# Attention scores: every product over 128 rows, the first block as two f32r products

## The chip, the cores and the metric

The kernel runs on one core of a Trainium2 chip. The metric is the time of the whole program on the device, in microseconds (us). Of three runs of the kernel before, the median was 1330.12 us (1329.44 to 1330.89).

## The reference, cut to what matters

Two layers, each with three token mixers on 512 tokens of width 1024. One of the mixers is a stick-breaking attention with 8 heads of 64 columns, in blocks of 128 queries; query block `blk` sees the keys of all blocks up to its own:

```python
def stick_breaking(q, k, v, q_norm, k_norm):
    q = rmsnorm(q, q_norm)
    k = rmsnorm(k, k_norm)
    for blk in range(S_ // SB_BLOCK):
        z = einsum('bqhd,bkhd->bhqk', q[:, start:end], k[:, :end]) * scale
        causal = s_idx[None, :] < t_idx[:, None]
        log_keep = where(causal, log_sigmoid(-z), 0.0)
        after = cumsum(log_keep, axis=3, reverse=True) - log_keep
        w = where(causal, exp(log_sigmoid(z) + after), 0.0)
        outs.append(einsum('bhqk,bkhd->bqhd', w, v[:, :end]))
```

The change concerns `z` alone, the scores.

## The kernel before, in words

**Main work.** The weights come as 196 units of 128 x 1024 floats. Each is split into a high part `wh` (ScalarE rounds it to f32r, L316) and a low part `wl` (VectorE subtracts, through the helper at L197), and the activations likewise (`hh`, `hl`). A product of matrices is then three f32r products per step: high by high, high by low, low by high. Nearly all main products (tile `mm`) have 128 rows, 128 stationary columns and 512 moving columns. They are issued in pieces of 24 products, in an order written out by hand.

**The order around the change.** Everything else is a set of generators that are advanced between or behind the pieces: at a piece's start those that are due go one step (ScalarE, VectorE and POOL work is issued there), then the piece's products are issued, and a generator that yielded 0 goes on behind the piece; there it issues its own products. Each engine works through its own queue in the order of issue. A budget per piece, counted from the columns of the products issued, decides how much background work (the preparation of the third mixer, on VectorE and POOL) is issued with it.

**The attention.** `sb_pair` treats two heads (a pair) whose 64 columns lie on rows 0 to 63 and 64 to 127 of the tiles `sq` and `sk` (named `sqk` in the trace). At its start it makes, for each head h: `qd[h]`, the high part of q, by ScalarE on the head's own 64 rows and copied by POOL (a cast, L1029) to the other 64 rows; `ks[h]`, the high part of k on the head's own rows (ScalarE) and the low part on the other rows (VectorE); and the low part of q in one tile `ql` for both heads, each on its own rows (VectorE). A product of `qd[h]` with `ks[h]` over all 128 rows is so q-high by k-high plus q-high by k-low; the product of `ql` with the high rows of `ks[h]`, over 64 rows, adds q-low by k-high. `scores` (L1032) does this for blocks 1 to 3. For block 0 it takes one plain float32 product of q and k over the head's 64 rows, which shows as two records. Behind each block's products a bf16 product of `identb` and `negm` adds -1e30 above the diagonal: the mask.

Per head the scores of block 3 are issued in one place (tile `z3`, with 512 columns of keys) and those of blocks 0, 2 and 1 one or two pieces later (`z02`, `z1`, with 128, 384 and 256 columns). `weights_of` turns the scores into weights: two sigmoids by ScalarE (`kp`, `w`), scans and a product by VectorE (L1051 and L197). `turn` transposes the weight blocks through TensorE (tile `wt`, L1068), ten per head; the first is from block 0, the second from block 1. The values are then added up in `sbo`, products with 64 output columns that alternate between the two heads' halves. Pairs start four pieces apart, so that the copies of one pair are made while the pair before it has the scores of its second head.

The trace names a product out<-moving,stationary. All tiles named z (`z3`, `z02`, `z1`) show as `z`.

Of the kernel before, what the change touches and what calls it, by code (L numbers as in the profile page):

```python
# [10 lines left out]
F32 = mybir.dt.float32  # L11
F32R = mybir.dt.float32r
BF16 = mybir.dt.bfloat16
AF = mybir.ActivationFunctionType
ALU = mybir.AluOpType
# [171 lines left out]
def trunk(ctx: ExitStack, tc, x_in, w_in, par_in, bc_in, ng_in, cst_in, rope_in, out):  # L187
    nc = tc.nc
    load = {"V": 0.0, "G": 0.0, "T": 0.0}

    def counted(f, engine, each):


        def g(*a, **k):
            o = k["out"] if "out" in k else a[0]
            load[engine] += 0.07 * (engine != "T") + each * math.prod(o.shape[1:])
            return f(*a, **k)  # L197

        return g

    TT = counted(nc.vector.tensor_tensor, "V", 1.04e-3)
# [4 lines left out]
    MM = counted(nc.tensor.matmul, "T", 0.42e-3)  # L206
# [9 lines left out]
    def bt(name, dt=F32, shape=(P, 512)):  # L216
        return bp.tile(list(shape), dt, tag="b", name=name)
# [7 lines left out]
    def psm(name):  # L225
        return ps_sm.tile([P, 512], F32, tag="sm", name=name)
# [12 lines left out]
    def C(n):  # L239
# [7 lines left out]
        out=negm, in_=negm, pattern=[[1, P]], base=0, channel_multiplier=-1, compare_op=ALU.is_ge, fill=0.0  # L247
# [31 lines left out]
    def split(src, name, shape=(P, 512)):  # L279
        h = bt(name + "h", F32R, shape)  # L280
        l = bt(name + "l", F32R, shape)
        ACT(h, src, AF.Copy)  # L282
        TT(out=l, in0=src, in1=h.bitcast(F32), op=ALU.subtract)
        return h, l
# [523 lines left out]
    def layer(l, last, base):  # L808
# [206 lines left out]
        def sb_pair(pr):  # L1015
            w02, w3 = [None] * 2, [None] * 2
            qf, kf = sq[pr], sk[pr]
            half = [slice(0, 64), slice(64, 128)]

            qd = [bt("qd0", F32R), bt("qd1", F32R)]  # L1020
            ks = [bt("ks0", F32R), bt("ks1", F32R)]
            ql = bt("ql", F32R)
            for h in range(2):
                r, o = half[h], half[1 - h]
                ACT(qd[h][r, :], qf[r, :], AF.Copy)  # L1025
                ACT(ks[h][r, :], kf[r, :], AF.Copy)
                TT(out=ql[r, :], in0=qf[r, :], in1=qd[h][r, :].bitcast(F32), op=ALU.subtract)
                TT(out=ks[h][o, :], in0=kf[r, :], in1=ks[h][r, :].bitcast(F32), op=ALU.subtract)
                nc.gpsimd.tensor_copy(out=qd[h][o, :], in_=qd[h][r, :])  # L1029
            yield K["b1"]  # L1030

            def scores(ps, off, h, b):  # L1032
                n = 128 * (b + 1)
                c = slice(b * P, b * P + P)
                r = half[h]
                if b == 0:
                    MM(ps[:, off : off + n], qf[r, c], kf[r, 0:n], start=True, stop=False)
                else:
                    MM(ps[:, off : off + n], qd[h][:, c], ks[h][:, 0:n], start=True, stop=False)
                    MM(ps[:, off : off + n], ql[r, c], ks[h][r, 0:n], start=False, stop=False)  # L1040
                MM(ps[:, off + n - P : off + n], identb, negm, start=False, stop=True)

            def weights_of(ps, segs, sg):

                end = sum(segs[-1])
                kp = bt("kp")
                ACT(kp[:, 0:end], ps[:, 0:end], AF.Sigmoid, scale=-0.125)  # L1047
                ACT(sg, ps[:, 0:end], AF.Sigmoid, scale=0.125)
                for off, n in segs:
                    v = kp[:, off + 1 : off + n][:, ::-1]  # L1050
                    nc.vector.tensor_tensor_scan(v, v, zero1.to_broadcast([P, n - 1]), 1.0, ALU.mult, ALU.add)  # L1051
                TT(out=sg[:, 0 : end - 1], in0=sg[:, 0 : end - 1], in1=kp[:, 1:end], op=ALU.mult)

            w1 = bt("w1")
            wt0, wt13, wt2 = [None] * 2, [None] * 2, bt("wt2")

            def wblk(h, b, kb):
                c = kb * P + (128 if b == 2 else 256 * h if b == 1 else 0)
                return (w02[h], w1, w02[h], w3[h])[b][:, c : c + P]

            def turn(h):
                pts = []
                for blocks in (
                    [(b, 0) for b in range(4)], [(1, 1), (2, 1), (3, 1), (3, 3)], [(2, 2), (3, 2)],
                ):
                    pt = psm("wt")
                    for i, (b, kb) in enumerate(blocks):
                        nc.tensor.transpose(pt[:, i * P : i * P + P], wblk(h, b, kb), ident)  # L1068
                    pts.append(pt)
                return pts  # L1070

            def turned(h, pts):
                wt0[h], wt13[h] = bt("wt0"), bt("wt13")
                ACT(wt0[h], pts[0], AF.Copy)
                nc.vector.tensor_copy(out=wt13[h], in_=pts[1])
                ACT(wt2[:, 256 * h : 256 * h + 256], pts[2][:, 0:256], AF.Copy)

            for h in range(2):
                ps = psm("z3")
                scores(ps, 0, h, 3)  # L1080
                if h == 1:
                    pts = turn(0)
                yield 0
                w3[h] = bt("w3")
                weights_of(ps, [(0, 512)], w3[h])
                if h == 1:
                    turned(0, pts)
                yield K["b2"]
                ps, ps1 = psm("z02"), psm("z1")
                scores(ps, 0, h, 0)  # L1090
                scores(ps, 128, h, 2)
                scores(ps1, 0, h, 1)
                yield 0
                w02[h] = bt("w02")
                weights_of(ps, [(0, 128), (128, 384)], w02[h])
                weights_of(ps1, [(0, 256)], w1[:, 256 * h : 256 * h + 256])
                yield K["b3"]
            pts = turn(1)
            yield 0
            turned(1, pts)  # L1100
            yield K["b4"]
            po = psm("sbo")
            for kb in range(4):

                for h in range(2):
                    c = slice(128 * pr + 64 * h, 128 * pr + 64 * h + 64)
                    w = (wt0[h], wt13[h][:, 0:384], wt2[:, 256 * h : 256 * h + 256], wt13[h][:, 384:512])[kb]
                    MM(po[half[h], 128 * kb : 512], sv[kb][:, c], w, start=kb == 0, stop=kb == 3)
            yield 0
            sbo[pr] = bt("sbo")  # L1110
            nc.vector.tensor_copy(out=sbo[pr], in_=po)
            yield K["b5"]
            while zb[pr] is None:
                yield 1
            TT(out=sbo[pr], in0=sbo[pr], in1=zb[pr], op=ALU.mult)
            yb[pr] = split(sbo[pr], "yb")
# [207 lines left out]
        for i in range(4):  # L1324
            spawn(sb_pair(i), at["sv"] + 3 + K["sb0"] + K["sb_gap"] * i)
# [66 lines left out]
```

## Time and profile before

| what | value |
|---|---|
| median of three runs | 1330.12 us |
| the profiled execution | 1332.1 us |
| its span in the profile | 1330.4 us |
| instructions | 16615 |
| TensorE busy | 1299.4 us, 6360 products |
| VectorE busy | 854.5 us |
| ScalarE busy | 537.7 us |
| POOL busy | 371.3 us |
| mean granted clock of TensorE | 0.993 |

The profile is of one execution, which took a little longer than its span and than the median of the runs. Busy times are shares of the span. The end of a product is modelled in the profile, so that records of products that follow each other overlap; the start of one to the start of the next is what TensorE spends on it. An idle time in brackets, as in [1.66 <-DVE w L197], is how long the engine stood still before that row, and what ended it.

### The profile page before, as it was taken

What the parts mean: (1) busy time and instruction counts of PE and PEld (TensorE: products, weight loads), DVE (VectorE), ACT (ScalarE), POOL (GpSimd) and SP (SyncE); (2) the same over time, 40 slices, a digit from 0 to 9 for tenths busy, and PEclk for the clock granted to TensorE, in tenths of its full rate; (3) what the DMA queues carried; (4) which work ended last, traced back from release to release, by engine and by line L of the source; (5) the groups of instructions that cost most, each with busy time, mean ns of one, the idle gap of its engine ahead of it and who ended that gap; (6) DMA issues with size and microseconds to landing.
All of it is one profiled execution on the core that took longest, in us unless ns stands there. A gap on an engine that the chain in (4) does not pass through costs nothing. (4 is left out here: it accounts for less than half of the span.)

```text
span 1330.4 us, 16615 instructions
## 1 busy us (share of the span) xinstructions
PE 1299.4 (98%) x6360; PEld 1051.4 (79%) x6360; DVE 854.5 (64%) x1189; ACT 537.7 (40%) x919; POOL 371.3 (28%) x436
## 2 busy tenths in 40 slices
PE   7989989999999999999999999899999999999998
PEld 5867768788887888888888777688888878888887
DVE  5996677886686438555365566779647854485542
ACT  5345543535434434333234444344544444333311
POOL 3330035738443012000052000575465321120000
PEclk9999989999999999999999999899999999999999
DMA  6232221223321222224533221112242233223342
GB/s 220 85 125 77 64 64 30 94 68 96 100 91 64 95 80 73 86 91 139 166 113 125 79 65 64 48 64 80 80 127 64 64 94 97 79 64 95 95 131 75
DMA packets 37375, 120.05 MB, mean 90 GB/s; under 512 B 4144, under 2 KB 4528, under 8 KB 37296
## 3 DMA queue, kind: packets, MB, share of 16 engines
q1 hardware_dynamic: 29664, 105.40, 25.2%
q10 hardware_dynamic: 7632, 13.59, 3.0%
q8 instruction: 50, 0.82, 0.3%
q14 instruction: 29, 0.24, 0.1%
HBM read 114.78 MB, written 4.19 MB: 89 GB/s over the span
## 5 line engine op out<-in xcount | busy, mean ns | idle before, releaser
L197 DVE TENSOR_TENSOR wl<-raw,wh 128x1024 fp32r<-128x1024 f32 x196 | 250.4, 1287 | 122.1 <-ACT wh L316 120.0
L197 PE MATMUL mm<-hh,wh 128*128 128x512 f32 x640 | 256.7, 401 | 0.0
L197 PE MATMUL mm<-hh,wl 128*128 128x512 f32 x640 | 252.4, 394 | 2.3 <-DVE wl L197 2.3
L197 PE MATMUL mm<-hl,wh 128*128 128x512 f32 x640 | 250.5, 391 | 0.0
L316 ACT ACTIVATE wh<-raw 128x1024 fp32r<-128x1024 f32 x196 | 206.0, 1057 | 86.1 <-DVE wl L197 31.1
L197 PE MATMUL mm<-wh,hh 128*128 128x512 f32 x512 | 210.2, 411 | 0.9 <-ACT hh L419 0.9
L197 PE MATMUL mm<-wl,hh 128*128 128x512 f32 x512 | 205.3, 401 | 4.1 <-DVE wl L197 4.1
L197 PE MATMUL mm<-wh,hl 128*128 128x512 f32 x512 | 204.7, 400 | 0.0
L197 PEld LDWEIGHTS mm<-hh,wl 128*128 128x128 f32 x640 | 120.6, 188 | 30.3 <-DVE wl L197 3.6
L197 PEld LDWEIGHTS mm<-hh,wh 128*128 128x128 f32 x640 | 120.8, 189 | 24.9 <-issue 1.8
L197 PEld LDWEIGHTS mm<-hl,wh 128*128 128x128 f32 x640 | 120.7, 189 | 24.5
L197 PEld LDWEIGHTS mm<-wl,hh 128*128 128x128 f32 x512 | 104.8, 205 | 25.7 <-DVE wl L197 6.8
L197 PEld LDWEIGHTS mm<-wh,hh 128*128 128x128 f32 x512 | 104.6, 204 | 21.3 <-ACT hh L419 1.3
L197 PEld LDWEIGHTS mm<-wh,hl 128*128 128x128 f32 x512 | 104.5, 204 | 20.9 <-DVE hl L197 0.3
L1051 DVE TENSOR_TENSOR_SCAN kp<-kp,zero 128x511 f32<-128x511 f32 (+1 forms) x64 | 60.3, 963 | 35.6 <-ACT kp L1047 35.1
L992 ACT ACTIVATE gate<-mm 128x512 f32<-128x512 f32 x48 | 28.6, 596 | 119.7 <-PE mm L197 119.7
L197 POOL TENSOR_SCALAR ms<-ss 128x8 f32<-128x8 f32 (+3 forms) x56 | 19.2, 342 | 184.0 <-DVE ss L822 101.9
L1029 POOL CAST qd<-qd 64x512 fp32r<-64x512 f32 x16 | 15.8, 988 | 186.9 <-ACT qd L1025 172.0
L197 POOL TENSOR_TENSOR rs<-ms,mhalf 128x8 f32<-128x8 f32 (+3 forms) x56 | 64.7, 1155 | 4.7
L820 ACT ACTIVATE sq<-mm 128x512 f32<-128x512 f32 x32 | 19.0, 593 | 89.1 <-PE mm L197 89.1
L197 PE MATMUL mm<-wl,mgh 128*128 128x512 f32 x128 | 50.1, 391 | 0.2
L197 PE MATMUL mm<-wh,mgh 128*128 128x512 f32 x128 | 49.9, 390 | 0.0
(254 smaller groups left out, 2260.4 us busy)
## 6 DMA issues: line engine op xcount, KB each, us to landing
raw<-in_w SPq DMA_DIRECT2D x196, 512.0 KB, 3.5
x<-in_x SPq DMA_DIRECT2D x8, 256.0 KB, 7.3
rope<-in_rope ACTq DMA_DIRECT2D x8, 256.0 KB, 4.3
xh<-in_x ACTq DMA_DIRECT2D x8, 256.0 KB, 4.6
x<-xh ACTq DMA_DIRECT2D x8, 256.0 KB, 2.1
xh<-x ACTq DMA_DIRECT2D x8, 256.0 KB, 4.5
out<-xh ACTq DMA_DIRECT2D x8, 256.0 KB, 2.1
gB<-in_ng SPq DMA_DIRECT2D x2, 256.0 KB, 5.8
```

What stands on the lines that cost most here:

```text
L197: return f(*a, **k)
L316: ACT(wh, raw, AF.Copy)
L820: ACT(s2, ps, AF.Square)
L992: ACT(sg, ps, AF.Sigmoid)
L1029: nc.gpsimd.tensor_copy(out=qd[h][o, :], in_=qd[h][r, :])
L1051: nc.vector.tensor_tensor_scan(v, v, zero1.to_broadcast([P, n - 1]), 1.0, ALU.mult, ALU.add)
```

## The change

Instead of one tile `ql` for both heads there are two, `ql[0]` and `ql[1]`. Each holds the head's low part of q on the head's own 64 rows, as before, and zeros on the other 64, which a memset on POOL writes, issued ahead of the cast of the same head. The second product of a block then goes over all 128 rows of `ql[h]` and `ks[h]`; the rows with the low part of k meet the zeros. Block 0 is treated like the others: the plain float32 product over 64 rows is replaced by the two f32r products over 128 rows, with 128 columns. The mask products, the weights and what follows stay.

```diff
             qd = [bt("qd0", F32R), bt("qd1", F32R)]
             ks = [bt("ks0", F32R), bt("ks1", F32R)]
-            ql = bt("ql", F32R)
+
+            ql = [bt("ql0", F32R), bt("ql1", F32R)]
             for h in range(2):
                 r, o = half[h], half[1 - h]
                 ACT(qd[h][r, :], qf[r, :], AF.Copy)
                 ACT(ks[h][r, :], kf[r, :], AF.Copy)
-                TT(out=ql[r, :], in0=qf[r, :], in1=qd[h][r, :].bitcast(F32), op=ALU.subtract)
+                nc.gpsimd.memset(ql[h][o, :].bitcast(F32), 0.0)
+                TT(out=ql[h][r, :], in0=qf[r, :], in1=qd[h][r, :].bitcast(F32), op=ALU.subtract)
                 TT(out=ks[h][o, :], in0=kf[r, :], in1=ks[h][r, :].bitcast(F32), op=ALU.subtract)
                 nc.gpsimd.tensor_copy(out=qd[h][o, :], in_=qd[h][r, :])
             yield K["b1"]
...
                 n = 128 * (b + 1)
                 c = slice(b * P, b * P + P)
-                r = half[h]
-                if b == 0:
-                    MM(ps[:, off : off + n], qf[r, c], kf[r, 0:n], start=True, stop=False)
-                else:
-                    MM(ps[:, off : off + n], qd[h][:, c], ks[h][:, 0:n], start=True, stop=False)
-                    MM(ps[:, off : off + n], ql[r, c], ks[h][r, 0:n], start=False, stop=False)
+                MM(ps[:, off : off + n], qd[h][:, c], ks[h][:, 0:n], start=True, stop=False)
+                MM(ps[:, off : off + n], ql[h][:, c], ks[h][:, 0:n], start=False, stop=False)
                 MM(ps[:, off + n - P : off + n], identb, negm, start=False, stop=True)
```

## Rows read from the trace of the kernel before

**Rows 1.** The page, part 1: busy time, share, instructions of three engines.

```profile
PE 1299.4 (98%) x6360; PEld 1051.4 (79%) x6360; DVE 854.5 (64%) x1189; ACT 537.7 (40%) x919; POOL 371.3 (28%) x436
```

**Rows 2.** The waits of TensorE: total us, times, longest us.

```profile
PE wt L1068 <- DVE w L197: 8.1, 4, 2.4
PE mm L197 <- DVE wl L197: 6.3, 7, 1.5
PE z L197 <- DVE ks L197: 2.7, 1, 2.7
```

**Rows 3.** TensorE's timeline (start, duration): scores of blocks 0, 2, 1 of a head.

```profile
115.69 0.40 PE L197 MATMUL mm<-hh,wl 128*128 128x512 f32 x1
116.02 0.48 PE L197 MATMUL z<-sqk 64*128 64x128 f32 x2
116.44 0.23 PE L197 MATMUL z<-negm,identb 128*128 128x128 bf16 x1
...
116.82 0.44 PE L197 MATMUL z<-ks,ql 64*128 64x384 f32 x1
117.20 0.23 PE L197 MATMUL z<-negm,identb 128*128 128x128 bf16 x1
...
117.53 0.38 PE L197 MATMUL z<-ks,ql 64*128 64x256 f32 x1
117.84 0.23 PE L197 MATMUL z<-negm,identb 128*128 128x128 bf16 x1
...
118.19 0.39 PE L197 MATMUL mm<-hl,wh 128*128 128x512 f32 x1
```

**Rows 4.** TensorE's timeline: scores of block 3, and the transposes behind them.

```profile
123.24 0.39 PE L197 MATMUL mm<-hh,wl 128*128 128x512 f32 x1
123.47 0.40 PE L197 MATMUL z<-ks,qd 128*128 128x512 f32 x1
123.80 0.49 PE L197 MATMUL z<-ks,ql 64*128 64x512 f32 x1
124.22 0.23 PE L197 MATMUL z<-negm,identb 128*128 128x128 bf16 x1
124.29 1.26 PE L1068 MATMUL wt<-ident,w 128*128 128x128 f32 x10
125.31 0.48 PE L197 MATMUL mm<-hh,wh 128*128 128x512 f32 x1
```

**Rows 5.** TensorE's timeline: f32r products of 256 columns in the retention.

```profile
1169.51 0.28 PE L197 MATMUL ro<-rvsh,sTs 128*128 128x256 f32 x1
1169.62 0.28 PE L197 MATMUL ro<-rvsl,sTs 128*128 128x256 f32 x1
1169.74 0.28 PE L197 MATMUL ro<-rvsh,sTs 128*128 128x256 f32 x1
```

**Rows 6.** The timeline of all engines: POOL's memsets beside a VectorE product.

```profile
217.26 0.99 POOL L767 MEMSET mt<- 128x512 f32 x2
...
217.67 0.68 DVE L197 TENSOR_TENSOR sbo<-sbo,silu 128x512 f32<-128x512 f32 x1
```

**Rows 7.** VectorE's timeline from a pair's copies to the previous pair's last weights.

```profile
117.27 0.68 DVE L197 TENSOR_TENSOR ql<-sqk,qd 64x512 fp32r<-64x512 f32 x1 [3.38 <-ACT qd L1025]
117.98 0.98 DVE L197 TENSOR_TENSOR ks<-sqk,ks 64x512 fp32r<-64x512 f32 x1
...
120.01 0.69 DVE L197 TENSOR_TENSOR ks<-sqk,ks 64x512 fp32r<-64x512 f32 x1
...
123.46 0.42 DVE L197 TENSOR_TENSOR w<-w,kp 128x255 f32<-128x255 f32 x1
```

**Rows 8.** TensorE's timeline at a wait for the weights `w`.

```profile
190.93 0.30 PE L1068 MATMUL wt<-ident,w 128*128 128x128 f32 x1 [1.66 <-DVE w L197]
```

**Rows 9.** Two stretches: busy us (instructions) of PE, PEld, DVE, ACT, POOL; granted clock.

```profile
190.00:200.00 10.00, 6.66 (x21) 5.65 (x22) 8.36 (x8) 1.98 (x5) 4.83 (x5) 0.66 0.29 97
415.00:425.00 10.00, 7.97 (x35) 5.95 (x35) 9.73 (x8) 4.02 (x5) 5.08 (x3) 1.00 0.50 161
```

## Prediction, made before the change was built

> **What bounds the kernel now.** I read the page's busy times first: TensorE is busy for 98% of the span, VectorE for 64% [rows 1]. A busy share alone says little, since the ends of products are modelled, so next come TensorE's own waits: it waits for VectorE's `w` four times, for `wl` seven times, for `ks` once, 17.1 us in all [rows 2]; beyond these it waits only for the first input, at the start. Outside these places the order of TensorE's queue is the clock of the program, and a product that gets shorter moves everything behind it forward. So the price of a score product is not its recorded duration but the distance from its start to the next start, and I read those distances in the timeline of TensorE.
>
> In a run of main products the distance is 0.23 us. The scores of blocks 0, 2 and 1 of one head stand in [rows 3], those of block 3 in [rows 4]. There the reader is to see that every change between a 128-row and a 64-row product lengthens a distance. Into one: the last main product to the first `sqk` product 0.33 (115.69 to 116.02), `qd` of 512 columns to `ql` 0.33 (123.47 to 123.80): 0.10 more than 0.23. Out of one: `ql` of 512 columns to the mask 0.42 (123.80 to 124.22), 0.19 more; the plain product of block 0 (two records) to the mask takes 0.42, of which 0.22 are left for the product if the way out is 0.20. Products of 128 rows on both sides don't pay it: two f32r products of 256 columns in the retention start 0.11 to 0.12 apart [rows 5], and ten transposes of 128 columns take 1.02 us, 0.10 each [rows 4].
>
> **The change, part by part.** There are 16 heads (2 layers, 4 pairs, 2 heads), each with its four blocks of scores and a mask behind each. All prices are per head.
>
> *Block 3.* `qd` to `ql` to mask is 0.33 + 0.42 = 0.75 [rows 4]; with no change of rows it is 2 x 0.23 = 0.46. Saved: 0.29.
>
> *Block 0.* The plain product goes, two f32r products of 128 rows and 128 columns come. Before: 0.33 + 0.42 = 0.75 from the last main product to the mask [rows 3]. After: 0.23 for the main product, then two products whose price no row has. The lower end is 0.06 each, half of the 256-column distance [rows 5]; the upper end is 0.21 each, what the plain product of this size takes (0.42 less the way out). I take 0.10, from the transposes, which also have 128 stationary columns and 128 moving ones [rows 4]. After 0.43, saved 0.32; ends 0.40 and 0.10.
>
> *Block 2, 384 columns.* Mask to `ql` is 0.38 now (116.44 to 116.82) [rows 3]. A mask followed by a 512-column product of 128 rows takes 0.35 to the start after it (117.84 to 118.19), and 384 columns are 0.055 shorter (halfway between 0.12 and 0.23): 0.295, saved 0.085. `ql` to mask falls from 0.38 to 0.175, saved 0.205.
>
> *Block 1, 256 columns.* Mask to `ql` 0.33 to 0.24, saved 0.09; `ql` to mask 0.31 to 0.12, saved 0.19 [rows 3, 5].
>
> Sum: 0.29 + 0.32 + 0.085 + 0.205 + 0.09 + 0.19 = 1.18 us per head, 18.9 us over 16 heads.
>
> The weak point is the change out: after every 64-row product comes a mask in bf16, so no row parts the change of rows from the change of type. If the 0.19 to 0.20 belonged to the mask, four of them would stay and 1.18 would become 0.39. I take the rows as the cause, since the change in costs 0.10 with no change of type. The Trainium skill, TensorEngine Tiling (Array Packing), section Key Properties, says that changing the tiling mode (not just the tile) drains the engine; by that rule both directions go and the sum is the 18.9, without it as little as 6.2.
>
> *The memsets.* 16 of them, 64 x 512, on POOL, ahead of the cast of the same head. The nearest row is a 128 x 512 memset, two in 0.99 us [rows 6], so about 0.5 us each, 8 us in all on an engine that is busy for 28% [rows 1]. The first of a pair needs no input and runs while POOL waits for ScalarE; the second puts the second cast back by 0.5 us. Cost on TensorE: 0, because the first product that reads the cast stands a whole main piece (5 us) behind it, and the memset of a head ends before its cast, for which that product waits already. If that cover is gone it is 0.5 us per pair, 4 us. Does a memset slow VectorE, whose `ks` of 0.69 us takes 0.98 while POOL casts [rows 7]? Beside the two memsets a VectorE product of two tiles took 0.68 us [rows 6], undisturbed. So 0; the upper end is 0.3 us in each of the six places below, 2 us. The Trainium skill has both answers: GPSIMD Engine Reference, section Specifications, names contention with VectorE instructions of two SBUF inputs without saying which POOL instructions; SBUF — State Buffer, section Who interferes with whom, leaves out those that only write. The row is with the second; by the first the sum would be up to 2 us smaller.
>
> The number of VectorE's subtractions and of ScalarE's copies stays. Two of the `ql` products per head get 64 zero rows, which no row prices; a product's distance goes by columns in [rows 3 to 5], so 0. The background's budget counts one more product of 128 columns per head, 0.05 us against pieces of 5: 0, either way at most one small operation moved.
>
> **What is late next.** In every layer three of the four pairs make their copies (`qd`, `ks`, `ql`) just when the previous pair's second head has its block-0, -2 and -1 scores. VectorE then runs a closed chain: it starts when ScalarE has made `qd`, right behind the main piece, and goes through four subtractions, the scans and ends with `w` at 123.88 (123.46 + 0.42) [rows 7]. The transposes that read it start at 124.29, the second of them (which needs this `w`) at 124.39 [rows 4]: about 0.43 us of slack. The chain's start hangs on the main piece, not on the scores, so TensorE comes 1.18 us earlier and waits 1.18 - 0.43 = 0.75. There are four such places, alike in the two layers: 3.0 us given back. At the last pair of each layer POOL's background runs beside this chain, and TensorE waits there already: two waits per layer, 8.1 us in all [rows 2], the first of them in [rows 8]. That is 1.18 more per layer, 2.4 us. The first block 3 of the first layer stands between waits for `ks` and `wl` [rows 2], set by VectorE: its 0.3 is lost. At the last head of each layer one of the waits for `wl` [rows 2] ends a VectorE chain that starts at the mask of block 2, so what is saved behind that mask, 0.3, is lost: 0.6. Given back: 3.0 + 2.4 + 0.3 + 0.6 = 6.3 us.
>
> Net: 18.9 - 6.3 = **12.6 us**. The profiled execution took 1332.1 us, 1.7 above its span and 2.0 above the median of the runs; it would be 1319.5, and the median 1330.1 - 12.6 = **1317.5 us**.
>
> **The rivals.**
> 1. Nothing is given back, because the chains start earlier too: 18.9, 1311.2 us. For it, most of the chains hang on TensorE; against it, VectorE's start behind ScalarE's `qd`. Chance 0.10.
> 2. The two f32r products of 128 columns cost what the plain one costs, 0.21 each: 0.96 per head, 15.4; given back 4 x 0.53 + 2 x 0.96 + 0.6 = 4.6; net 10.8, 1319.3 us. For it, that no f32r product under 256 columns stands in the trace. Chance 0.15.
> 3. The change out belongs to the mask: 0.39 per head, 6.2; the four places have slack enough, the two waits and the first block take 0.9; net 5.3, 1324.8 us. Chance 0.11.
> 4. Slower: the clock falls at the new waits. At the existing one the granted clock over 10 us is 0.66 [rows 9] (a mix of its two levels, 2.4 GHz as 1.0 and 1.2 GHz as 0.5); that loses between 0.34 x 6.66 busy us = 2.3 and 0.34 x 10 = 3.4 us, say 2.9. At four new places that is 11.6, 1329.1 us (chance 0.01); at all six 17.4 us against 12.6, 1334.9 us (chance 0.04). It decides from 2.1 us per place on. Against it: in a stretch with waits for `wl` (the longest 1.5 us [rows 2]), where TensorE was busy for only 7.97 of 10 us, the clock stayed at 1.00 [rows 9], and the new waits are 0.75 us.
> 5. The change doesn't do what it says: the lengthening comes from two products with the same `ks` following each other into one bank, and stays. Against it, the retention's products also add up in one bank, 0.12 apart [rows 5]. About 1330 us, chance 0.04.
>
> **How the numbers follow.** My forecast has 0.55, with 1313 to 1321 us of its own: 0.06 or 0.21 for the 128-column product, nothing or all of the 2 us of contention, waits of 0.5 or 1.0 us. The range of 1310.5 to 1326 takes in rivals 1 to 3 with theirs and leaves out 4 and 5 and some tails. A run of this kernel can tell 0.2% (2.7 us) from no change. Faster by more: 0.55 + 0.10 + 0.15 + 0.11 = 0.91; within: rival 5 and the four-place case, 0.05; slower: 0.04.
>
> **What would show it.** In the profile after: `qd` to `ql` to mask of block 3 in 0.23 + 0.23; main product, `qd`, `ql`, mask of block 0 in 0.43; the stretch from 115.69 to 118.19, 2.50 us now [rows 3], in 1.6. TensorE waiting for `w` at six places instead of two, some 5 us longer in all. POOL with 16 more memsets of 0.5 us and no wait of TensorE for POOL. I am wrong on the cause if `ql` to mask stays above 0.3 us, on the give-back if no new wait for `w` shows, and on the sign if the granted clock falls in new places.

## The result, and the profile after

The changed kernel takes 1317.36 us (median of 4 runs, 1316.90 to 1318.61) beside 1330.17 us for the kernel before on the same chip: a ratio of 0.9905 with an interval of 0.9888 to 0.9922, which is 10.4 to 14.9 us less, 12.8 by the medians. The forecast was 1317.5 us, 12.6 less.

The profiled execution took 1317.28 us, with a span of 1315.6, which is 14.8 under the profiled span of before. Of these, 1.03 us are there before any changed instruction runs: at the start of the program the two executions stand that far apart. A second profiled execution of the changed kernel had a span of 1316.7. A distance between two traces is thus good to about 1 us in all, and what follows is read from places, not from spans.

Page, part 1, which answers to [rows 1]:

```profile
PE 1279.7 (97%) x6360; PEld 1048.5 (80%) x6360; DVE 853.2 (65%) x1189; ACT 538.4 (41%) x919; POOL 383.2 (29%) x452
```

TensorE has as many instructions as before, since a plain product of block 0 counted as two and is now two f32r products. POOL has 16 more, and is busy for 12 us more: 8.3 for the memsets, 0.52 each, and the rest because its other work takes longer in sum.

TensorE's waits, which answer to [rows 2] (total us, times, longest us):

```profile
PE wt L1066 <- DVE w L197: 13.2, 8, 3.0
PE mm L197 <- DVE wl L197: 9.2, 8, 3.3
```

The waits for `w` went from 4 to 8, two at the last pair of each layer as before and one at each of four new places. That is 5.1 us more, where "some 5" were forecast. The wait for `ks` is gone, and the longest wait for `wl` has grown from 1.5 to 3.3 us; this was not forecast.

TensorE's timeline (start, duration) of one head's blocks 0, 2 and 1, which answers to [rows 3], and of block 3 with its transposes, which answers to [rows 4]:

```profile
112.83 0.39 PE L197 MATMUL mm<-hh,wl 128*128 128x512 f32 x1
113.06 0.22 PE L197 MATMUL z<-ks,qd 128*128 128x128 f32 x1
113.11 0.28 PE L197 MATMUL z<-ks,ql 128*128 128x128 f32 x1
113.23 0.23 PE L197 MATMUL z<-negm,identb 128*128 128x128 bf16 x1
113.27 0.42 PE L197 MATMUL z<-ks,qd 128*128 128x384 f32 x1
113.53 0.34 PE L197 MATMUL z<-ks,ql 128*128 128x384 f32 x1
113.71 0.23 PE L197 MATMUL z<-negm,identb 128*128 128x128 bf16 x1
113.75 0.36 PE L197 MATMUL z<-ks,qd 128*128 128x256 f32 x1
113.95 0.28 PE L197 MATMUL z<-ks,ql 128*128 128x256 f32 x1
114.07 0.23 PE L197 MATMUL z<-negm,identb 128*128 128x128 bf16 x1
...
114.43 0.40 PE L197 MATMUL mm<-hl,wh 128*128 128x512 f32 x1
...
119.70 0.40 PE L197 MATMUL z<-ks,qd 128*128 128x512 f32 x1
119.94 0.39 PE L197 MATMUL z<-ks,ql 128*128 128x512 f32 x1
120.17 0.23 PE L197 MATMUL z<-negm,identb 128*128 128x128 bf16 x1
120.24 0.28 PE L1066 MATMUL wt<-ident,w 128*128 128x128 f32 x1
121.11 1.20 PE L1066 MATMUL wt<-ident,w 128*128 128x128 f32 x9 [0.59 <-DVE w L197]
122.06 0.48 PE L197 MATMUL mm<-hh,wh 128*128 128x512 f32 x1
```

Three readings. The stretch of blocks 0, 2 and 1 runs from 112.83 to 114.43, 1.60 us for the 2.50 of before. Block 3 goes from product to product in 0.24 and 0.23, for 0.33 and 0.42. And behind it stands one of the new waits: the second transpose starts 0.87 after the first. Ten transposes and the way to the next main product take 1.82 us, for 1.02 before; 0.80 is given back here.

A table of how far each group of the trace of after is ahead of the same group of before, and by how much that lead changes, gives the account. I matched the groups by order and took the differences of their starts:

| place | forecast, us | trace, us |
|---|---|---|
| 16 heads, shorter distances | +18.9 | +19.0 (16 x (0.80 blocks 0, 2, 1 + 0.29 block 3 + 0.10 way in)) |
| four new waits for `w` | -3.0 | -3.4 (0.81, 0.87, 0.81, 0.87) |
| two old places of waits for `w` | -2.4 | -1.5 (1.37 and 1.39 lost, 0.60 and 0.62 of it won back until the next scores) |
| first pair of layer 1, besides the 0.29 of its block 3 | -0.3 | +0.4 |
| waits for `wl` at the last heads | -0.6 | -0.7 (0.33, 0.37) |
| sum | +12.6 | +13.8 |

With the 1.03 us of the start that is the 14.8 between the spans.

Granted clock. A stretch with a new wait, and the first old place (length, then busy us of PE, PEld, DVE, ACT, POOL with instructions; granted clock; DMA share; GB/s):

```profile
118.00:130.00 12.00, 11.41 (x61) 8.67 (x61) 8.92 (x13) 6.43 (x12) 0.52 (x1) 1.00 0.29 87
185.00:195.00 10.00, 7.43 (x27) 6.73 (x28) 7.59 (x8) 0.98 (x2) 4.06 (x4) 0.66 0.19 52
```

The new wait leaves the clock at 1.00 (so does the second, from 147 to 160 us). At the old place it falls to the same 0.66 as in [rows 9], so as much of the 10 us is low as before. But the low stretch now begins earlier in the order of the work. From the first main product behind the transposes to the next scores, in the kernel before and in the changed one:

```profile
195.48:203.22 7.74, 7.74 (x27) 6.64 (x25) 3.07 (x4) 0.38 (x1) 0.00 (x0) 0.73 0.24 68
189.70:196.75 7.05, 7.05 (x27) 6.47 (x25) 3.08 (x4) 0.38 (x1) 0.00 (x0) 0.80 0.27 74
```

The same products stand there, and they take 0.69 us less: 0.09 is the way into the scores, and the other 0.60 is what the table calls won back. While the clock is low these products are 0.43 apart, for 0.23 to 0.24 at full clock, and in the changed kernel three fewer of them are that far apart.

### The profile page after: what moved, and what is told of

The parts are those of the page before. It is cut to its first block, busy times and chain, and to the rows that moved or that the text cites. A ratio compares the mean times of both kernels' runs of the same rounds, so it can differ in the third digit from the quotient of the medians.

```text
span 1315.6 us, 16640 instructions
## 1 busy us (share of the span) xinstructions
PE 1279.7 (97%) x6360; PEld 1048.5 (80%) x6360; DVE 853.2 (65%) x1189; ACT 538.4 (41%) x919; POOL 383.2 (29%) x452
## 5 line engine op out<-in xcount | busy, mean ns | idle before, releaser
L1049 DVE TENSOR_TENSOR_SCAN kp<-kp,zero 128x511 f32<-128x511 f32 (+1 forms) x64 | 67.3, 1071 | 26.1 <-ACT kp L1045 26.0
```

## The experiments

### The plain product of block 0 put back

```
+                r = half[h]
+                if b == 0:
+                    MM(ps[:, off : off + n], qf[r, c], kf[r, 0:n], start=True, stop=False)
+                else:
+                    MM(ps[:, off : off + n], qd[h][:, c], ks[h][:, 0:n], start=True, stop=False)
+                    MM(ps[:, off : off + n], ql[h][:, c], ks[h][:, 0:n], start=False, stop=False)
```

> Blocks 1 to 3 go over 128 rows, block 0 keeps the plain product over 64 rows. Theory (every change of rows costs TensorE about 0.1 us in and 0.2 us out, VectorE's chain gives back only what exceeds its slack of 0.43 us): of the 1.18 us per head the 0.35 of block 0 are missing, 0.83 x 16 = 13.3 us; given back 4 x 0.40 + 2 x 0.83 = 3.3; with the 0.7 us that the first pair gains beside it, some 1319.5 us, and the stretch from the last main product to the second one behind the scores of blocks 0, 2 and 1 takes 1.95 us. Waits for w at six places, the four new ones near 0.3 us. Rival (the plain float32 product is what costs, the rows of the others do not matter): the time stays within 3 us of 1330.

Measured: 1319.61 us (1318.26 to 1321.67), ratio 0.9917 (0.9902 to 0.9931), where the theory had 1319.5. TensorE's timeline:

```profile
112.83 0.48 PE L197 MATMUL z<-sqk 64*128 64x128 f32 x2
113.24 0.23 PE L197 MATMUL z<-negm,identb 128*128 128x128 bf16 x1
```

The 64-row product keeps its 0.41 us to the mask, in a kernel in which every other product has 128 rows, and the other blocks keep their new distances. A head saves 0.55 to 0.57 at blocks 2 and 1 and 0.29 at block 3; the new waits cost 0.46 to 0.54 each.

### Block 0 alone changed

The products with `ql` of blocks 1 to 3 take 64 rows again:

```
+                r = half[h] if b else slice(0, P)
                 MM(ps[:, off : off + n], qd[h][:, c], ks[h][:, 0:n], start=True, stop=False)
-                MM(ps[:, off : off + n], ql[h][:, c], ks[h][:, 0:n], start=False, stop=False)
+                MM(ps[:, off : off + n], ql[h][r, c], ks[h][r, 0:n], start=False, stop=False)
```

> Only block 0 becomes two f32r products over 128 rows; blocks 1 to 3 keep their second product over 64 rows. The memsets are there. Theory: 0.35 x 16 = 5.6 us saved; at the four places with slack 0.43 nothing is given back, at the two places with a wait 0.35 each; with the first pair's 0.7 some 1324.5 us, and waits for w at the two old places only. So the two parts alone would save more together than the whole change (about 10.7 + 5.6 against 12.8), because the slack is used twice. Rival (what is given back is a share of what is saved, wherever it comes from): 30% of 12.8, 1326.3 us, and the parts add up to the whole.

Measured: 1325.68 us (1323.94 to 1327.09), ratio 0.9961 (0.9947 to 0.9975). The time stands between both expectations and decides nothing; the trace does. TensorE's timeline at block 2:

```profile
115.14 0.44 PE L197 MATMUL z<-ks,ql 64*128 64x384 f32 x1
115.52 0.23 PE L197 MATMUL z<-negm,identb 128*128 128x128 bf16 x1
```

A head saves 0.34, and TensorE waits for `w` four times, at the old places alone. So the four new places had a slack of about 0.34 at least, and a saving up to it is kept whole. The two halves of the change save 11.0 and 4.9 us, together 15.9 where the whole saves 12.8. Not all of this is slack that is used twice. In the traces the halves together are 3.9 us ahead of the whole: 1.3 at the four new places (which lose 3.4 in the whole, 2.0 and nothing in the halves), 0.7 at the first pair, whose gain both halves have, and 1.9 at the last pairs of the layers, where the clock is not low for equally long in all of these executions (0.79 from 184 to 200 us in the changed kernel, 0.89 with block 0 plain). The slack is shown by the places, not by the sum. The rows also part two things that the prediction could not. Behind a 64-row product the mask stands 0.38 later (115.14 to 115.52); behind a 128-row product with the same columns, in the changed kernel, 0.18 (113.53 to 113.71). Both times the type changes from f32r to bf16, so the 0.20 is for the rows.

### Changes of rows counted, with no product changed

The kernel before, with the products of blocks 2 and 1 in another order: both `qd`, both `ql`, both masks.

```
+            def scores21(ps, ps1, h):
...
+                    MM(p[:, off : off + n], qd[h][:, c], ks[h][:, 0:n], start=True, stop=False)
...
+                    MM(p[:, off : off + n], ql[r, c], ks[h][r, 0:n], start=False, stop=False)
...
+                    MM(p[:, off + n - P : off + n], identb, negm, start=False, stop=True)
...
-                scores(ps, 128, h, 2)
-                scores(ps1, 0, h, 1)
+                scores21(ps, ps1, h)
```

> The kernel before, with the products of blocks 2 and 1 in another order: both qd products, then both 64-row ql products behind each other, then both masks. The number of 64-row products and their work stays; the array goes from 128 to 64 rows and back once less per head. Theory (the price hangs on the change of rows): about 0.1 + 0.2 us per head less, some 0.3 x 16 = 5 us, of which the two waits take 0.6: 1326 us; the two ql products stand side by side at 0.17 and then 0.3 us. Rival (a 64-row product is slow in itself, or the mask behind any product is): within 1.5 us of 1330.

Measured: 1325.52 us (1324.79 to 1326.98), ratio 0.9962 (0.9947 to 0.9976). TensorE's timeline at blocks 2 and 1:

```profile
116.89 0.44 PE L197 MATMUL z<-ks,ql 64*128 64x384 f32 x1
117.17 0.28 PE L197 MATMUL z<-ks,ql 64*128 64x256 f32 x1
117.38 0.28 PE L197 MATMUL z<-negm,identb 128*128 128x128 bf16 x2
```

All 64-row products are still there; only one way in and one way out per head are gone, and a head is 0.34 to 0.36 shorter. The price hangs on the changes of rows and not on the number of 64-row products. Of it, 0.07 is the order itself, with one change of type fewer, which the last runs of this section measure with 128-row products alone; 0.28 is left for one way in and one way out.

Where the 0.28 stands was not as expected (0.17 between the two `ql`, then 0.3 to the mask). The distances are 0.28 and 0.21, for 0.18 and 0.12 behind 128-row products of the same columns in the changed kernel above. So 0.10 stands between two 64-row products, where no rows change, and only 0.09 on the way out. What is shown is the price of going to 64 rows and back, once for a group of products; the split into 0.10 in and 0.20 out holds for a single product, and no run here settles why it shifts.

### The zeros written by ScalarE

```
-                nc.gpsimd.memset(ql[h][o, :].bitcast(F32), 0.0)
+                ACT(ql[h][o, :], qf[o, :], AF.Copy, scale=0.0)
```

> The zeros are written by ScalarE (a copy times zero, 64 x 512) instead of by POOL; all else as after the change. Theory: the memsets cost TensorE nothing, and only in the first pair of the first layer did they help, because a memset leaves VectorE alone where POOL otherwise reads: the four VectorE operations ahead of ql take 0.7 to 1.3 us again instead of 0.35 to 0.65, and the first pair comes about 0.7 to 1 us later. ScalarE's 0.6 us per head lie behind its copies and end before VectorE reaches the scans: nothing. Time 1317.4 + 0.8 = 1318.2 us, between 1317 and 1320. Rival (the memsets slow VectorE's chain): 2 us faster, 1315.5.

Measured: 1319.45 us (1318.86 to 1320.06), ratio 0.9914 (0.9899 to 0.9929). That is in the theory's range, and not faster, as the rival had it. Without the memsets on POOL the first pair of layer 1 is about 0.4 us later, and its wait for `ks` is back with 2.2 us. That fits memsets that had helped there, against the forecast, and asked for the next run. (Of the 2.1 us to the changed kernel this is the smaller part: 0.6 stands at the four new places, the rest at the start and at the last pairs, where two executions of the changed kernel differ by as much.)

### The memsets three times

```
                 nc.gpsimd.memset(ql[h][o, :].bitcast(F32), 0.0)
+                nc.gpsimd.memset(ql[h][o, :].bitcast(F32), 0.0)
+                nc.gpsimd.memset(ql[h][o, :].bitcast(F32), 0.0)
```

> Each of the 16 memsets is issued three times. POOL's casts then come 1 us later per head, its background 2 us later per pair. Theory (memsets write only and contend with nothing, the casts have a main piece of slack): no more than 1 us from 1317.4 either way; VectorE's subtractions beside memsets take 0.69 us. Rival (POOL's queue or its contention is on the path): 2 x 1 us more for each pair that is late, 4 to 16 us, 1321 or more.

Measured: 1312.76 us (1311.66 to 1312.93), ratio 0.9862 (0.9847 to 0.9877). It is 4.6 us faster than the changed kernel, whose ratio was 0.9905 (0.9888 to 0.9922), and both theories fall. In the trace 3.5 us come from the first pair of layer 1, and about 0.8 from the last pair of each layer. VectorE's timeline at that first pair, in the changed kernel:

```profile
87.78 1.44 DVE L197 TENSOR_TENSOR ql<-sqk,qd 64x512 fp32r<-64x512 f32 x1
89.25 1.64 DVE L197 TENSOR_TENSOR ks<-sqk,ks 64x512 fp32r<-64x512 f32 x1
```

The same with the memsets three times:

```profile
88.16 0.69 DVE L197 TENSOR_TENSOR ql<-sqk,qd 64x512 fp32r<-64x512 f32 x1
88.88 0.69 DVE L197 TENSOR_TENSOR ks<-sqk,ks 64x512 fp32r<-64x512 f32 x1
```

POOL's timeline there, in the changed kernel:

```profile
87.28 1.39 POOL L197 TENSOR_TENSOR ct<-bi,co_re 128x512 f32<-128x512 f32 x1
88.74 1.59 POOL L197 TENSOR_TENSOR bbi<-ct,ct 128x512 f32<-128x512 f32 x1
```

With the memsets three times:

```profile
90.12 1.92 POOL L197 TENSOR_TENSOR ct<-bi,co_re 128x512 f32<-128x512 f32 x1
```

In the changed kernel POOL's background product `ct` and difference `bbi` run beside VectorE's `ql` and `ks`, which take 1.44 and 1.64 us. The extra memsets put POOL's background behind them, and they take 0.69 each. It doesn't vanish: the four `wl` behind them, which it now runs beside, take 7.32 us for 5.53. But TensorE's wait for the first of these falls from 3.27 to 1.45, and the granted clock rises. The stretch from 87 to 100 us, in the changed kernel:

```profile
87.00:100.00 13.00, 9.73 (x39) 7.22 (x38) 11.18 (x9) 5.94 (x8) 6.14 (x6) 0.87 0.47 153
```

With the memsets three times:

```profile
87.00:100.00 13.00, 11.55 (x55) 8.96 (x54) 12.68 (x12) 8.84 (x14) 11.43 (x12) 1.00 0.44 158
```

The shorter wait is 1.8 us, 0.13 of the clock over 13 us are 1.7, and the sum is the 3.5.

### The same delay, by work that reads

Two copies ahead of each memset, in place of the two more memsets:

```
+                for _ in range(2):
+                    nc.gpsimd.tensor_copy(out=ql[h][o, :], in_=qf[o, :])
                 nc.gpsimd.memset(ql[h][o, :].bitcast(F32), 0.0)
```

> Two copies by POOL that read the scores' query tile go ahead of each memset, in place of the two extra memsets; POOL's later work is held back about as long as with the memsets three times, but now by work that reads. Theory (VectorE's two-input operations are slowed by what POOL reads, and memsets help because they put nothing but writes there): the subtraction and the copies of the first pair beside them take 1 us or more, not 0.69; the first pair gains under 1 us or loses up to 1, and the time is 1316 to 1319 us. Rival (only the order matters: POOL's background comes later, whatever holds it back): the first pair gains its 3 us in each layer as with the memsets, and the time is 1311.5 to 1314 us.

It ran beside the changed kernel once more, of which was expected:

> The changed kernel once more, as the mark that the other two are held against on one chip: 1317.4 us, within 1.5.

Measured: the changed kernel 1318.51 us (1316.87 to 1318.69), as expected; with the copies 1314.59 (1313.33 to 1316.89), ratio to the kernel before 0.9889 (0.9872 to 0.9906). The two intervals overlap (0.9896 to 0.9926 for the changed kernel beside it), so what follows rests on the traces. The theory had foreseen durations right and time wrong. VectorE's `ql` of the first pair take 1.09 and 0.99:

```profile
86.73 1.09 DVE L197 TENSOR_TENSOR ql<-sqk,qd 64x512 fp32r<-64x512 f32 x1
87.86 0.98 DVE L197 TENSOR_TENSOR ks<-sqk,ks 64x512 fp32r<-64x512 f32 x1
88.88 0.99 DVE L197 TENSOR_TENSOR ql<-sqk,qd 64x512 fp32r<-64x512 f32 x1
89.89 0.69 DVE L197 TENSOR_TENSOR ks<-sqk,ks 64x512 fp32r<-64x512 f32 x1
```

These four take 3.8 us from the first start to the last end, 4.8 in the changed kernel and 3.1 with the memsets three times: of the 1.7 us that the memsets three times take off, 1.0 comes from the order (POOL's long products come behind VectorE's chain) and 0.7 from the memset's not reading.

The first pair of layer 1 gains 1.9 us on the first execution of the changed kernel and 1.6 on the second, between the theory's under 1 and the rival's 3. Only 0.3 of it are shorter waits (0.90 for `ks` and 1.90 for `wl`, where the changed kernel has 3.27 for `wl`). The rest is the clock, which does not fall here, as with the memsets three times:

```profile
87.00:100.00 13.00, 10.20 (x48) 7.62 (x47) 12.68 (x10) 7.23 (x13) 12.45 (x11) 1.00 0.39 126
```

What the copies read costs elsewhere: TensorE waits for `w` twelve times instead of eight, and each of the four new places loses about 0.7 us more. At the last pair of each layer the later background makes the waits 3.0 us shorter, for 1.0 with the memsets; 0.4 and 1.0 of that are lost again in the main products behind them. Neither theory holds alone. The time, just above the rival's range, owes more to the last pairs, which neither had in its sum, than to the first. The layer 2 part of the rival's expectation was mistaken: there POOL has no background at the first pair, and nothing is won.

### The copies of pairs 1 to 3 one piece earlier

If the new waits come from VectorE's chain, which starts behind ScalarE's `qd`, they must go when the copies start one main piece earlier:

```
-            yield K["b1"]
+            yield K["b1"] + (pr > 0)
...
-            spawn(sb_pair(i), at["sv"] + 3 + K["sb0"] + K["sb_gap"] * i)
+            spawn(sb_pair(i), at["sv"] + 3 + K["sb0"] + K["sb_gap"] * i - (i > 0))
```

> After the change, with the copies of pairs 1 to 3 issued one piece earlier (their scores stay where they are), so that they no longer stand ahead of the scans of the previous pair's last weights in VectorE's queue. Theory (VectorE's closed chain, four subtractions and then the scans, gives back what is saved): the four new waits for w vanish, 4 x 0.8 = 3.3 us, and the two long ones (3.04 + 2.41 us each) shrink by at least the 3.4 us of the subtractions or go altogether; about 3.3 + 2 x (3.4 to 5.4) = 10 to 14, and up to 2 x 2.9 us more where the granted clock no longer falls: 1298 to 1308 us, 1305 the likeliest. Rival (the waits come from POOL's reads beside the scans, or from ScalarE): the four may go, the two long ones stay, 1314 us or more.

> The kernel before, with the same earlier copies. Theory: only the two places with waits (4.07 us each) have something to give, the other four have slack already: 2 x (3 to 4) us and up to 2 x 2.9 us for the clock, 1317 to 1324 us, and the change then saves nearly its whole 18.9 us between this kernel and the one before it in this list. Rival (what is given back has nothing to do with the copies): the difference between these two kernels stays at 12.8 us.

Measured: with the change 1308.86 us (1307.02 to 1309.34), ratio 0.9832 (0.9817 to 0.9847); without it 1323.86 (1323.57 to 1325.61), ratio 0.995 (0.9935 to 0.9965). TensorE's waits for `w`, with the change:

```profile
PE wt L1066 <- DVE w L197: 5.4, 4, 2.0
```

Its timeline where the first new wait stood:

```profile
120.24 1.26 PE L1066 MATMUL wt<-ident,w 128*128 128x128 f32 x10
```

The ten transposes run in one piece again, and each of the four places wins back its 0.81 to 0.87. That shows the cause of the new waits: the copies stood ahead of the scans in a chain of VectorE that has no idle time (114.40 to 121.05 in the changed kernel, 6.65 us; 117.27 to 123.88 and 6.61 before). With the early copies the change is worth 15.0 us; between the two traces every head again differs by 0.80, 0.29 and 0.10. That is more than the rival's 12.8, but not nearly the whole 18.9 that was expected: 2.1 and 2.3 us are lost at the last pairs of the two layers, where the waits are longer with the change and the clock falls (0.89 from 184 to 200 us, 1.00 without the change), 0.7 at the waits for `wl` of the last heads, and 1.4 is won at the first pair. The time with the change was forecast too low, the likeliest at 1305 us, and lies 0.9 us above the range: the last pairs won 3.1 us in layer 1 and 2.3 in layer 2, and their waits are still there, 1.96 and 0.74 us in each. POOL's casts move forward too, and with them its background, which now runs beside VectorE's scans. POOL's timeline of this kernel:

```profile
173.24 1.61 POOL L197 TENSOR_TENSOR ab<-ab,ct 128x512 f32<-128x512 f32 x1
174.81 1.99 POOL L197 TENSOR_TENSOR ab<-bbr,y_re 128x512 f32<-128x512 f32 x1
```

VectorE's timeline in the same stretch:

```profile
173.64 2.30 DVE L1049 TENSOR_TENSOR_SCAN kp<-kp,zero 128x511 f32<-128x511 f32 x1
```

The same scan takes 1.21 where POOL is idle (at 185.79 in this trace), and the product behind it 0.69 for 1.30.

### The parts put together

The early copies with the products of blocks 2 and 1 side by side (all of 128 rows now), and then with the memsets three times as well:

> The change, the earlier copies and the grouped order of blocks 2 and 1 (qd, qd, ql, ql, mask, mask, all over 128 rows). Theory: with 128 rows everywhere grouping has no change of rows to save; only the load of the stationary block behind a short mask is exposed once less, some 0.05 us per head, 1 us in all beside the kernel with earlier copies alone. Rival (the order itself matters as it did in the kernel before): 5 us less than that kernel.

> The change, the copies one piece earlier, the query products of a block side by side, and every memset three times, together. Theory (the first pair is held by VectorE's operations beside POOL's reads, which the early copies do not touch since the first pair's copies stay where they were): 3 us at the first pair of each layer come off as with the memsets three times alone, less at the long waits, since these are already shorter: 1301 to 1304 us against 1307.6 for the early and grouped version. Rival (with the casts moved forward POOL is late already, and holding it back further makes the casts and the background late for the last pairs): 1306 to 1311 us.

Measured: 1307.55 us (1306.94 to 1308.79), ratio 0.9826 (0.9811 to 0.9841), and 1304.04 (1303.61 to 1304.86), ratio 0.9805 (0.9791 to 0.9820). With nothing but 128-row products the order of them is worth 0.06 to 0.08 us a head, near the theory's 0.05, where it was worth 0.34 to 0.36 with 64-row products in between. The memsets three times bring 3.7 us at the first pair of layer 1 here too, nothing at that of layer 2, and nothing at the long waits of layer 1, where the wait for the first `w` takes back the 0.5 that is won just before it. Behind those of layer 2 the last kernel is 1.5 us later. That is the clock. Around these waits, first without the memsets three times, then with them:

```profile
820.00:832.00 12.00, 9.53 (x46) 8.55 (x45) 10.11 (x11) 4.13 (x7) 3.65 (x4) 1.00 0.25 89
820.00:832.00 12.00, 10.94 (x49) 9.09 (x51) 6.39 (x9) 2.89 (x10) 1.31 (x3) 0.86 0.29 89
```

Without them the clock fell behind the long waits of layer 1 (0.89 from 184 to 200 us) and not behind those of layer 2, which are as long; no run here settles why. That is the theory where it spoke of layer 1, and in part the rival for the rest, since the waits of the last pairs grow by 0.6; the time meets the upper end of the theory's range. The last kernel is the fastest here, 14.5 us under the changed kernel of the same chip. Its ratio overlaps that of the one without the extra memsets, so the 3.5 us between those two rest on the traces.

## Why the prediction was right, and where it was not

**What bounds it.** The rule that TensorE's distances are the clock of the program held: 16 equal gains of 1.19 us can be followed through the trace, and each wait takes a countable part of them.

**The change of rows.** 0.10 in and 0.19 to 0.20 out were read right, and the choice of the rows over the mask as the cause of the way out is shown by blocks 2 and 1 above: rival 3 falls, and with it rival 5, since the lengthening went where only the rows changed. A single 64-row product pays both, 0.28 to 0.30 in all; two side by side pay 0.28 together, and not at the same two places. The Trainium skill, TensorEngine Tiling (Array Packing), section Key Properties, says that a change of the tiling mode drains the engine; the trace agrees in both directions, and prices it at 0.10 and 0.20 us around a single product here.

**Block 0** was right in its sum (0.40 for 0.43 from the last main product to the mask) but not in its terms: the two f32r products of 128 columns are 0.06 and 0.12 us apart from what follows, not 0.10 each. Rival 2, with 0.21 each, falls. (Its sum left out the 0.3 of the first block 3; with it the net is 10.5, not 10.8.) Blocks 2 and 1 came out at 0.30 and 0.18, and 0.24 and 0.12, as worked out.

**The four new waits** were right in place and cause and mis-sized by 0.1 us each, 0.81 and 0.87 for 0.75. Up to the transpose that waits, 0.75 and 0.81 are lost, so the slack was 0.44 and 0.38, for 0.43; 0.06 more goes on the distance behind it (0.17 to the next transpose, for 0.11). The undone half (block 0 alone), whose 0.34 a head fit into that slack, and the early copies show that it was slack of VectorE's chain. Rival 1 falls.

**The two old places** were sized too high. The term was 1.18 each; 1.37 to 1.39 were lost at the waits themselves, but 0.6 of it came back before the next scores, all of it in main products that ran at low clock before and at full clock now (the two stretches shown above; 0.6 in layer 2 as well). The prediction had no term for that, and it is the least steady place of the trace: in the main products behind the wait of layer 2 alone the second execution of the changed kernel is 1.1 us later than the first. What sets the start of the low stretch, no run here shows.

**The first pair** is the step that failed. "Cost on TensorE: 0" for the memsets and "its 0.3 is lost" for the first block 3 were both wrong, in sign. The prediction asked whether a memset slows VectorE; it did not ask what the memset holds back. VectorE's last four operations ahead of `ql` had taken 3.98 us together, two beside POOL's casts and two beside its `ct` and `bbi`. With a memset of 0.5 us ahead of each cast they stand beside memsets and one cast, `ct` comes behind them, and they take 1.71 (2.88 with the zeros written by ScalarE). The last two of them and POOL's work beside them, in the kernel before:

```profile
87.17 1.11 DVE L197 TENSOR_TENSOR dbl<-ci,cr 128x192 f32<-128x192 f32 x1
88.32 1.34 DVE L197 TENSOR_TENSOR ci<-dbl,dbl 128x192 f32<-128x192 f32 x1
87.01 1.07 POOL L197 TENSOR_TENSOR ct<-bi,co_re 128x512 f32<-128x512 f32 x1
88.16 1.29 POOL L197 TENSOR_TENSOR bbi<-ct,ct 128x512 f32<-128x512 f32 x1
```

The same two in the changed kernel (`ct` at 87.28, as shown above), and POOL's second memset:

```profile
85.09 0.65 DVE L197 TENSOR_TENSOR dbl<-ci,cr 128x192 f32<-128x192 f32 x1
85.77 0.36 DVE L197 TENSOR_TENSOR ci<-dbl,dbl 128x192 f32<-128x192 f32 x1
85.58 0.52 POOL L1028 MEMSET ql<- 64x512 f32 x1
```

The wait for `ks`, 2.7 us in [rows 2], went with it. The `wl` behind the second pair of copies then became the wait (3.27 us for 1.02), which is why only 0.4 us were left of it.

**The clock** (rival 4) did not fall at the new waits, as forecast: 1.00 over the stretch shown. That it falls at the long ones cuts both ways, as the memsets three times showed, where a wait that became 1.8 us shorter gave 1.7 us more through the clock.

**The size.** The account above has 1.2 us more than the forecast, the medians 0.2 us more. The misses are +0.1, -0.4, +0.9, +0.7 and -0.1 us; they partly cancel, and the agreement of the medians to 0.2 us is better than the terms: that part is luck.

## What to carry to other kernels

A short product of fewer rows between products of full rows is priced by the changes of rows around it, here 0.10 us in and 0.20 out, so count the changes and not the products: pad it with zeros, or put such products side by side. Before a saving on a full engine is added up, look for the chains on other engines that do not start with it; each has a slack that is used up once, after which the rest is given back, and an earlier start of the chain wins that back (0.81 to 0.87 us a place here). Before two executions are compared by their times, look at the granted clock behind the long waits: here it moved a place by up to 1.5 us. And an instruction added to an engine that is far from busy is not free or dear by its own time only: ask what it moves behind, and beside which work that then runs.

## What the runs showed of the hardware

Work that is added to POOL made this kernel faster: 32 memsets more, 0.52 us each, took 4.6 us off (ratio 0.9862 for 0.9905). Half of the 3.5 us at the first pair is the granted clock, 1.00 for 0.87. VectorE's two-input operations pay for what POOL reads beside them. The second `ks` of layer 2's first pair takes 0.99 us beside POOL's cast, 0.69 where the memsets three times stand beside it in its place, and 0.98 where the copies do. The Trainium skill, SBUF — State Buffer, section Who interferes with whom, has VectorE instructions with two SBUF inputs contend with POOL instructions that read and not with those that only write; these three rows agree. The rule does not give sizes, and they go far: two scans, of 127 and of 383 columns, which take 1.27 us together beside no work of POOL, took 3.06 beside its products of two tiles. But not every pair pays alike, and no run here settles why: in the changed kernel `ql` took 0.69 beside a cast whose next neighbour `ks` took 0.99.

An f32r product of 128 columns behind a main product starts the next one 0.06 us later, and the second of the pair takes 0.12, as much as one of 256 columns in front of its mask. A product's distance there is no longer that of its columns alone.
